# Score passes of two maps taken alternately, each in its own bank, and the dilated heads two at a time

## The chip, the cores and the metric

The kernel runs on one core of one Trainium2 chip. The metric is device time in microseconds (us) of one execution. Five engines work side by side and are told apart by their names in the profile: PE (TensorE, with PEld for its weight loads), DVE (VectorE), ACT (ScalarE), POOL (GpSimd) and SP (SyncE, which issues DMAs).

## The reference, cut to what matters

Two transformer blocks over 512 tokens of width 1024, in fp32. The first block holds, beside a feed-forward part, eight heads of ordinary causal attention ("mla" in the kernel) and eight "dilated" heads of width 64. The second block runs two layers; each has four heads of differential attention, where a head has two score maps of width 64 whose softmaxes are subtracted.

```python
def dilated_attention(q, k, v):              # 8 heads of 64, first block
    ...
    for window, dil in DIL_PATTERNS:         # the kernel folds the patterns into one additive mask
        ...
    w = jax.nn.softmax(jnp.stack(lses, axis=0), axis=0)
    out = jnp.sum(w[..., None] * jnp.stack(outs, axis=0).astype(jnp.float32), axis=0)
...
def diff_attention(q, k, v, lq1, lk1, lq2, lk2, subln_g, rel_bias, lam_init):   # 4 heads x 2 maps of 64, each layer
    ...
        logits = jnp.einsum('bqhmd,bkhmd->bhmqk', qb, k).astype(f32) + bias
        logits = jnp.where(dist >= 0, logits, NEG_INF_2)
        p = jax.nn.softmax(logits, axis=-1)
        attn = p[:, :, 0] - lam * p[:, :, 1]
        return jnp.einsum('bhqk,bkhe->bqhe', attn.astype(v.dtype), v)
```

## The kernel before

**Products in three passes.** An fp32 operand is split into a high part and the rest (`hi` and `lo`, `qh` and `ql`, `th` and `tl`), and a product is the sum of three matmuls: high by high, and high by low twice. L414 issues these three passes for one block of scores; L202 to L204 and L183 to L185 do the same for the linear layers.

**Scores.** The 512 queries are taken in four blocks of 128 (`i` = 0 to 3); block `i` needs the scores against the first 128(i+1) keys, so a pass has 128, 256, 384 or 512 columns. `softmax_block` takes a PSUM bank from a pool of two (`psc`), issues the three passes of one map into it, lets DVE add the mask and take the row maximum out of the bank (L417, `z<-psc`, which frees the bank), and then has ACT take the exponential. A dilated head has its q and k in 64 rows: `th` and `tl` hold two heads, the first in rows 0 to 63, the second in rows 64 to 127. A differential head holds its two maps in the same way. So these passes contract over 64 rows and use one half of the rows of the array (the profile prints 64*128 where a full matmul is 128*128). The mla heads contract over 96 rows.

**The order of work.** `attention` walks through the heads one after the other and through the four blocks of each; one step `b` issues the scores of block `b`, the transposes of the probabilities of block `b - 3` (`put_pt`, L430) and, one step later, the products with the values (`values`, L455) of a finished head. `weave` puts pieces of other work between the steps at given rates ("fill": projections, and sums for a modulation vector, `adacc`). In the first block the 16 heads are eight dilated ones and then eight mla ones; the 32 dilated steps lie at 134 to 245 us of the trace, the mla steps at 245 to 330 us. In the second block the four differential heads of a layer lie at 1133 to 1236 us and at 2051 to 2152 us, each step with both maps. The order of instructions on an engine is set by a scheduler when the program is built, from the order in the code and its own idea of when a bank or an input is ready; on the chip each engine's queue then has that order.

**Names.** `psc` score bank, `pmm` bank of the linear layers, `ptr` transposes, `po` values, `z` a block's scores in SBUF, `pt` transposed probabilities (two buffers for the dilated and mla heads), `lo<-raw,hi` the low parts of a weight piece (L161, on DVE or POOL), `relm` and `kc` the masks.

Of the kernel before, what the change touches and what calls it, by code (L numbers as in the profile page):

```python
# [18 lines left out]
P = 128  # L19
# [384 lines left out]
            self.x = [self.done[n] for n in (1, 5, 6, 2, 7, 3, 4)]  # L404


def softmax_block(net, mats, i, mask, scale):

    nc = net.nc
    n = (i + 1) * P  # L410
    q = slice(i * P, i * P + P)
    ps = net.ps_sc()
    for j, (l, r) in enumerate(mats):
        nc.tensor.matmul(ps[:, :n], l[:, q], r[:, :n], start=(j == 0), stop=(j == len(mats) - 1))  # L414
    z = net.zp.tile([P, T], F32, tag="z", name="z")
    nm, s = net.tiny(1, "nm"), net.tiny(1, "s")
    nc.vector.tensor_tensor_reduce(out=z[:, :n], in0=ps[:, :n], in1=mask[:, T - n:], scale=-scale, scalar=BIG,  # L417
                                   op0=ALU.add, op1=ALU.min, accum_out=nm)
    nc.scalar.activation(out=z[:, :n], in_=z[:, :n], func=AF.Exp, scale=-1.0, bias=nm, accum_out=s)
    r = net.tiny(1, "r")  # L420
    nc.vector.reciprocal(out=r, in_=s)
    return z, r
# [37 lines left out]
def mats3(qh, ql, kh, kl):  # L460
    return [(qh, kh), (qh, kl), (ql, kh)]


def attention(net, heads):


    n = NB * len(heads)
    zs, ends = {}, []
    for b in range(n + LAG + VLAG):
        if b == 0:  # L470
            heads[0].prepare()
        if b % NB == NB - 1 and b < n - 1:
            heads[b // NB + 1].prepare()
        if b < n:
            zs[b] = heads[b // NB].scores(b % NB)
        c = b - LAG
        if 0 <= c < n:
            h = heads[c // NB]
            if c % NB == 0:
                h.pt = h.new_pt()  # L480
            put_pt(net, zs.pop(c), c % NB, *h.pt)
        c -= VLAG
        if c >= 0 and c % NB == NB - 1:
            ends.append(heads[c // NB].output())
        for e in ends:
            next(e, None)
        yield
    for e in ends:
        for _ in e:
            pass  # L490
# [32 lines left out]
class Head64:  # L523
# [3 lines left out]
    def __init__(self, net, prep, mask, scale, v, out, then=None):  # L527
        self.net, self.prep, self.mask, self.scale, self.v, self.out = net, prep, mask, scale, v, out
        self.then = then

    def prepare(self):
        self.mats = self.prep()

    def scores(self, i):
        nc = self.net.nc
        z, r = softmax_block(self.net, self.mats, i, self.mask, self.scale)
        n = (i + 1) * P
        if i in ON_DVE:
            nc.vector.tensor_scalar(out=z[:, :n], in0=z[:, :n], scalar1=r, scalar2=None, op0=ALU.mult)
        elif i in SCALE_POOL:  # L540
            nc.gpsimd.tensor_tensor(out=z[:, :n], in0=z[:, :n], in1=r.to_broadcast([P, n]), op=ALU.mult)
        else:
            nc.scalar.activation(out=z[:, :n], in_=z[:, :n], func=AF.Identity, scale=r)
        return z
# [289 lines left out]
def first_body(net):  # L834
# [64 lines left out]
    with ExitStack() as c2:  # L899
# [295 lines left out]
        def shared_keys():  # L1195
# [4 lines left out]
            for kh, kl in ks:  # L1200
# [4 lines left out]

        net.share = SHARE[0]
        half1 = 4 * NB - 1
        weave(attention(net, dilated(0) + dilated(1) + mla(ks)),
              (half1, chain(dil_keys(1), dil_values(1)), RATES[0],
               mods, ADA_RATES[0]),  # L1210
              (half1 + 1, chain(mla_queries(), mla_keys(), shared_keys()), RATES[1], mods, ADA_RATES[1]),
# [225 lines left out]
class HeadDiff:  # L1437
# [6 lines left out]
    def new_pt(self):  # L1444
        return new_pt(self.net)

    def prepare(self):
        pass

    def scores(self, i):  # L1450
        net, nc = self.net, self.net.nc
        n = (i + 1) * P
        ms = []
        for m in range(2):
            r = slice(64 * m, 64 * m + 64)
            ms.append(softmax_block(net, mats3(*(t[r, :] for t in self.qk())), i, self.masks[:, m, :], 1.0))
        (z0, r0), (z1, r1) = ms
        nc.vector.tensor_scalar(out=r1, in0=r1, scalar1=self.nlam, scalar2=None, op0=ALU.mult)
        nc.scalar.activation(out=z1[:, :n], in_=z1[:, :n], func=AF.Identity, scale=r1)
# [24 lines left out]
def mixer(net, l, x, norm, M, nlam, gsub, sp8, nsp8, wl):  # L1484
# [37 lines left out]
    def da():  # L1522
        hs = []
        for hh in range(4):
# [8 lines left out]
                return vs[hp][0][kb // 2][:, c], vs[hp][1][kb // 2][:, c]  # L1533

            hs.append(HeadDiff(net, lambda hh=hh: qk["q", hh] + qk["k", hh], M[hh], nlam, v, out))
        return attention(net, hs)

    def scaled(c0, name, out):
        for j, ps in net.lin_fm(W[:, c0:c0 + 256], KD, 256, x):
# [199 lines left out]
```

## Time and profile before

| | |
|---|---|
| median of three executions | 2595.83 us (2595.31 to 2596.23) |
| profiled execution | 2595.03 us, of which the span of the trace is 2593.2 us |
| PE busy | 2512.7 us, 97% of the span |
| DVE busy | 1903.2 us, 73% |
| ACT busy | 1214.8 us, 47% |
| POOL busy | 269.2 us, 10% |
| mean granted TensorE clock | 0.986 of full speed |

The page's busy times are unions of instruction spans. A matmul's span reaches to the end of its results, while the next one starts earlier, so PE counts as busy also where it only drains; how close PE is to its limit has to be read from the distances between the starts of its matmuls.

### The profile page before, as it was taken

What the parts mean: (1) busy time and instruction counts of PE and PEld (TensorE: products, weight loads), DVE (VectorE), ACT (ScalarE), POOL (GpSimd) and SP (SyncE); (2) the same over time, 40 slices, a digit from 0 to 9 for tenths busy, and PEclk for the clock granted to TensorE, in tenths of its full rate; (3) what the DMA queues carried; (4) which work ended last, traced back from release to release, by engine and by line L of the source; (5) the groups of instructions that cost most, each with busy time, mean ns of one, the idle gap of its engine ahead of it and who ended that gap; (6) DMA issues with size and microseconds to landing.
All of it is one profiled execution on the core that took longest, in us unless ns stands there. A gap on an engine that the chain in (4) does not pass through costs nothing.

```text
span 2593.2 us, 38138 instructions
## 1 busy us (share of the span) xinstructions
PE 2512.7 (97%) x15288; PEld 2188.8 (84%) x15288; DVE 1903.2 (73%) x2860; ACT 1214.8 (47%) x1804; POOL 269.2 (10%) x246
## 2 busy tenths in 40 slices
PE   5999989999989999999999999999999999999998
PEld 4886768788879999887789999799998877899998
DVE  8788786555578877656688777788776566897775
ACT  4367644233355444445455444554444455544443
POOL 3256320000000000022200000000000222000000
PEclk9999989999999999999999999999999999999999
DMA  8432253333223333331223333233333421233332
GB/s 254 121 105 71 78 152 102 123 97 94 79 80 114 98 103 101 113 115 50 73 82 106 99 107 98 74 118 103 104 106 98 122 66 52 76 117 98 106 110 70
DMA packets 318774, 261.62 MB, mean 101 GB/s; under 512 B 10203, under 2 KB 310619, under 8 KB 318596
## 3 DMA queue, kind: packets, MB, share of 16 engines
q1 hardware_dynamic: 313184, 250.98, 31.4%
q10 hardware_dynamic: 5412, 8.20, 1.0%
q8 instruction: 120, 1.97, 0.3%
q14 instruction: 58, 0.48, 0.1%
HBM read 257.03 MB, written 4.74 MB: 101 GB/s over the span
## 4 chain that ended last, share of the span: by engine, by line
PE 49%; DVE 2%; ACT 1%; POOL 1%; issue 0%; DMA 0%; DVEq 0%; POOLq 0%; ACTq 0%; SPq 0%
PE ptr L183 4%; PE ptr L184 4%; PE ptr L185 4%; PE pmm L245 4%; PE pmm L247 4%; PE pmm L246 4%; PE pmm L183 3%; PE pmm L185 3%; PE pmm L184 3%; PE po L245 2%; PE po L246 2%; PE po L247 2%; PE psc L247 2%; PE psc L246 2%; PE psc L245 2%; PE pmm L203 1%
## 5 line engine op out<-in xcount | busy, mean ns | idle before, releaser
L157 ACT ACTIVATE hi<-raw 128x1024 fp32r<-128x1024 f32 (+3 forms) x434 | 448.0, 1033 | 545.5 <-PE pmm L184 171.1
L161 DVE TENSOR_TENSOR lo<-raw,hi 128x1024 fp32r<-128x1024 f32 (+2 forms) x402 | 482.4, 1201 | 219.4 <-ACT hi L157 213.6
L247 PE MATMUL pmm<-gh,lo 128*128 128x256 f32 x1344 | 378.8, 282 | 5.7 <-DVE lo L161 5.6
L245 PE MATMUL pmm<-gh,hi 128*128 128x256 f32 x1344 | 379.9, 283 | 3.1 <-ACT hi L157 2.5
L246 PE MATMUL pmm<-gl,hi 128*128 128x256 f32 x1344 | 378.3, 282 | 0.0
L183 PE MATMUL ptr<-uh,hi 128*128 128x512 f32 x832 | 330.2, 397 | 0.2 <-ACT hi L157 0.2
L184 PE MATMUL ptr<-ul,hi 128*128 128x512 f32 x832 | 329.3, 396 | 0.0
L185 PE MATMUL ptr<-uh,lo 128*128 128x512 f32 x832 | 329.0, 395 | 0.0
L253 POOL TENSOR_TENSOR rp<-var,neghalf 128x4 f32<-128x4 f32 (+2 forms) x46 | 56.8, 1236 | 1989.8 <-DVE var L258 1989.6
L245 PEld LDWEIGHTS pmm<-gh,hi 128*128 128x128 f32 x1344 | 258.4, 192 | 5.5 <-ACT hi L157 3.1
L247 PEld LDWEIGHTS pmm<-gh,lo 128*128 128x128 f32 x1344 | 254.0, 189 | 6.6 <-DVE lo L161 6.6
L246 PEld LDWEIGHTS pmm<-gl,hi 128*128 128x128 f32 x1344 | 254.3, 189 | 1.1
L183 PEld LDWEIGHTS ptr<-uh,hi 128*128 128x128 f32 x832 | 156.7, 188 | 37.4 <-ACT inv L308 0.8
L185 PEld LDWEIGHTS ptr<-uh,lo 128*128 128x128 f32 x832 | 156.3, 188 | 37.8
L184 PEld LDWEIGHTS ptr<-ul,hi 128*128 128x128 f32 x832 | 156.5, 188 | 35.9
L245 PE MATMUL po<-gh,hi 128*128 128x256 f32 x640 | 179.6, 281 | 1.7 <-ACT hi L157 1.7
L246 PE MATMUL po<-gl,hi 128*128 128x256 f32 x640 | 179.2, 280 | 0.0
L247 PE MATMUL po<-gh,lo 128*128 128x256 f32 x640 | 179.1, 280 | 0.0
L183 PE MATMUL pmm<-hh,hi 128*128 128x512 f32 x400 | 160.6, 403 | 6.2 <-ACT hh L761 3.3
L185 PE MATMUL pmm<-hh,lo 128*128 128x512 f32 x400 | 160.5, 402 | 3.8 <-DVE lo L161 3.8
L184 PE MATMUL pmm<-hl,hi 128*128 128x512 f32 x400 | 160.1, 401 | 0.0
L157 ACT ACTIVATE hi<-s 128x1024 fp32r<-128x1024 f32 x72 | 76.6, 1064 | 171.1 <-PE ptr L184 114.5
(411 smaller groups left out, 5841.4 us busy)
## 6 DMA issues: line engine op xcount, KB each, us to landing
raw<-in_ffn_gate SPq DMA_DIRECT2D x88, 512.0 KB, 3.6
raw<-in_ffn_up SPq DMA_DIRECT2D x88, 512.0 KB, 3.6
raw<-in_ffn_down SPq DMA_DIRECT2D x64, 512.0 KB, 3.4
raw<-in_w_in SPq DMA_DIRECT2D x60, 512.0 KB, 3.8
raw<-in_w_up SPq DMA_DIRECT2D x44, 512.0 KB, 3.8
wa<-in_w_ada SPq DMA_DIRECT2D x80, 256.0 KB, 3.0
raw<-in_ffn_down SPq DMA_DIRECT2D x32, 384.0 KB, 3.4
raw<-in_w_down SPq DMA_DIRECT2D x16, 512.0 KB, 3.4
```

What stands on the lines that cost most here:

```text
L157: nc.scalar.activation(out=hi, in_=v, func=AF.Copy)
L161: e.tensor_tensor(out=lo, in0=v, in1=hi.bitcast(F32), op=ALU.subtract)
L183: mm(ps, hi[:, k, c], xh, start=(k == 0), stop=False)
L184: mm(ps, hi[:, k, c], xl, start=False, stop=False)
L185: mm(ps, lo[:, k, c], xh, start=False, stop=(k == kt - 1))
L203: mm(ps[:, :n], xh[:, c], lo[:, k % kp, :], start=False, stop=False)
L245: mm(o, hi[:, k, c], xh[:, k, :], start=first, stop=False, skip_group_check=True)
L246: mm(o, hi[:, k, c], xl[:, k, :], start=False, stop=False, skip_group_check=True)
L247: mm(o, lo[:, k, c], xh[:, k, :], start=False, stop=(j == 1 and k == 3), skip_group_check=True)
L253: self.nc.gpsimd.tensor_tensor(out=r, in0=v, in1=self.neghalf[:, :n], op=ALU.pow)
```

## The change

`products` is new: it takes one bank for each map that it is given, and issues the first pass of every map, then the second pass of every map, then the third. `softmax_block` now gets a bank that is already filled. `attention` gets groups of heads in place of heads: a group's blocks are walked through together (block 0 of each head, then block 1 of each, ...), and all banks of the group's block are taken and filled at the step of its first head. A differential head is a group by itself with two maps; an mla head is a group by itself with one; the dilated heads form four groups of two. Number of passes, softmaxes, transposes and products with the values stay as they are, and so do the number of steps and the fill given to each.

```diff
-def softmax_block(net, mats, i, mask, scale):
+def products(net, i, *mats):
+
+
+    n = (i + 1) * P
+    q = slice(i * P, i * P + P)
+    banks = [net.ps_sc() for _ in mats]
+    for j, passes in enumerate(zip(*mats)):
+        for ps, (l, r) in zip(banks, passes):
+            net.nc.tensor.matmul(ps[:, :n], l[:, q], r[:, :n], start=(j == 0), stop=(j == len(mats[0]) - 1))
+    return banks
+
+
+def softmax_block(net, ps, i, mask, scale):
 
     nc = net.nc
     n = (i + 1) * P
-    q = slice(i * P, i * P + P)
-    ps = net.ps_sc()
-    for j, (l, r) in enumerate(mats):
-        nc.tensor.matmul(ps[:, :n], l[:, q], r[:, :n], start=(j == 0), stop=(j == len(mats) - 1))
     z = net.zp.tile([P, T], F32, tag="z", name="z")
...
-def attention(net, heads):
-
-
-    n = NB * len(heads)
+def attention(net, groups):
+
+
+
+    items = [(g, h, i) for g in groups for i in range(NB) for h in g]
+    later = dict(zip(groups, groups[1:]))
+    n = len(items)
     zs, ends = {}, []
+    for h in groups[0]:
+        h.prepare()
     for b in range(n + LAG + VLAG):
-        if b == 0:
-            heads[0].prepare()
-        if b % NB == NB - 1 and b < n - 1:
-            heads[b // NB + 1].prepare()
         if b < n:
-            zs[b] = heads[b // NB].scores(b % NB)
+            g, h, i = items[b]
+            if i == NB - 1 and h is g[-1]:
+                for other in later.get(g, ()):
+                    other.prepare()
+            if h is g[0]:
+                banks = products(net, i, *chain(*(o.maps() for o in g)))
+                for o in g:
+                    o.banks, banks = banks[:o.n_maps], banks[o.n_maps:]
+            zs[b] = h.scores(i)
         c = b - LAG
         if 0 <= c < n:
-            h = heads[c // NB]
-            if c % NB == 0:
+            _, h, i = items[c]
+            if i == 0:
                 h.pt = h.new_pt()
-            put_pt(net, zs.pop(c), c % NB, *h.pt)
+            put_pt(net, zs.pop(c), i, *h.pt)
         c -= VLAG
-        if c >= 0 and c % NB == NB - 1:
-            ends.append(heads[c // NB].output())
+        if c >= 0 and items[c][2] == NB - 1:
+            ends.append(items[c][1].output())
...
-        weave(attention(net, dilated(0) + dilated(1) + mla(ks)),
+        pairs = lambda hs: list(zip(hs[::2], hs[1::2]))
+        weave(attention(net, pairs(dilated(0)) + pairs(dilated(1)) + [(h,) for h in mla(ks)]),
...
+    def maps(self):
+        return [mats3(*(t[64 * m:64 * m + 64, :] for t in self.qk())) for m in range(2)]
...
-        ms = []
-        for m in range(2):
-            r = slice(64 * m, 64 * m + 64)
-            ms.append(softmax_block(net, mats3(*(t[r, :] for t in self.qk())), i, self.masks[:, m, :], 1.0))
+        ms = [softmax_block(net, self.banks[m], i, self.masks[:, m, :], 1.0) for m in range(2)]
...
-        return attention(net, hs)
+        return attention(net, [(h,) for h in hs])
```

What it does to the order of PE and DVE stands below at three places; the number behind a name tells buffers apart.

PE, second block, first layer, first differential head, 512 columns. Before, the three passes of map 0 into one bank and then those of map 1 into the other, in one piece:

```order
L414 MATMUL psc_10830<-kh_10479,qh_10436 128x512
L414 MATMUL psc_10830<-kl_10480,qh_10436 128x512
L414 MATMUL psc_10830<-kh_10479,ql_10437 128x512
L414 MATMUL psc_10841<-kh_10479,qh_10436 128x512
L414 MATMUL psc_10841<-kl_10480,qh_10436 128x512
L414 MATMUL psc_10841<-kh_10479,ql_10437 128x512
```

After:

```order
L415 MATMUL psc_10830<-kh_10479,qh_10436 128x512
L415 MATMUL psc_10831<-kh_10479,qh_10436 128x512
L415 MATMUL psc_10830<-kl_10480,qh_10436 128x512
L415 MATMUL psc_10831<-kl_10480,qh_10436 128x512
L415 MATMUL psc_10830<-kh_10479,ql_10437 128x512
L415 MATMUL psc_10831<-kh_10479,ql_10437 128x512
```

The six passes stood together before and stand together now; only the order among them has changed.

PE, first block, dilated stage, third head (the first of the second pair). Before, its block of 256 columns and, after three transposes, its block of 384; the fourth head's blocks stand about 80 rows further down:

```order
L414 MATMUL psc_1750<-th_1620,th_1611 128x256
L414 MATMUL psc_1750<-tl_1621,th_1611 128x256
L414 MATMUL psc_1750<-th_1620,tl_1612 128x256
L430 MATMUL ptr_1762<-ident_110,z_1592 128x128 x3
L414 MATMUL psc_1767<-th_1620,th_1611 128x384
L414 MATMUL psc_1767<-tl_1621,th_1611 128x384
L414 MATMUL psc_1767<-th_1620,tl_1612 128x384
```

After, the third and the fourth head's blocks of 256 columns in two banks, with the transposes and the values behind them:

```order
L415 MATMUL psc_1760<-th_1621,th_1612 128x256
L415 MATMUL psc_1761<-th_1621,th_1612 128x256
L415 MATMUL psc_1760<-tl_1622,th_1612 128x256
L415 MATMUL psc_1761<-tl_1622,th_1612 128x256
L415 MATMUL psc_1760<-th_1621,tl_1613 128x256
L415 MATMUL psc_1761<-th_1621,tl_1613 128x256
L438 MATMUL ptr_1776<-ident_110,z_1625 128x128 x4
L463 MATMUL po_1782<-pt_1422,vd_1072 64x512
```

Each head's three passes were a piece of their own; now the six passes of two heads are one piece, and the next block of the same head no longer stands right behind.

DVE, first block, dilated stage, fifth head, in the mla queries' fill. Before, the read of the head's second bank (`psc_2222`, 256 columns), with what stands ahead of it:

```order
L1093 TENSOR_SCALAR vr6_2161<-ss9_2159 128x3
L726 TENSOR_TENSOR sw_2170<-pmm_2144,g_mla_q_pe_s_588 128x3x16
L1091 TENSOR_SCALAR vr6_2161<-vr6_2161 128x3
L726 TENSOR_TENSOR sw_2170<-pmm_2144,g_mla_q_pe_s_588 128x3x16
L417 ISA z_2226,nm_2227<-psc_2222,kc_605 128x256
L417 ISA nm_2227 128x1
```

After, the read of the bank that the sixth head's first block has taken beside the fifth's (`psc_2120`), with what stands ahead of and behind it; the fifth head's bank (`psc_2119`) is read 13 rows earlier:

```order
L1115 TENSOR_SCALAR vr6_2157<-ss9_2155 128x3
L748 TENSOR_TENSOR sw_2166<-pmm_2140,g_mla_q_pe_s_588 128x3x16
L1113 TENSOR_SCALAR vr6_2157<-vr6_2157 128x3
L748 TENSOR_TENSOR sw_2166<-pmm_2140,g_mla_q_pe_s_588 128x3x16
L161 TENSOR_TENSOR lo_2181<-raw_2178,hi_2180 128x576
L1129 TENSOR_TENSOR t1_2164<-t1_2164,sw_2166 128x3x32
L425 ISA z_2218,nm_2219<-psc_2120,kc_605 128x128
L425 ISA nm_2219 128x1
L161 TENSOR_TENSOR lo_2384<-raw_2381,hi_2383 128x768
```

The read of the pair's second bank now stands behind a low-part subtraction (`lo`) and the fill's small steps, 13 rows behind the read of its first, and both banks are needed for the pair's next block.

## Rows read from the trace of the kernel before

**Rows 1.** Page, part 1: engine, busy us, share of the span, instructions.

```profile
PE 2512.7 (97%) x15288; PEld 2188.8 (84%) x15288; DVE 1903.2 (73%) x2860; ACT 1214.8 (47%) x1804; POOL 269.2 (10%) x246
```

**Rows 2.** Windows: stretch and length in us, busy us of each engine, PEclk, DMA share, GB/s.

```profile
134.00:245.00 111.00, 108.92 (x654) 84.12 (x653) 91.38 (x339) 75.37 (x188) 72.48 (x103) 1.00 0.29 93
160.00:220.00 60.00, 59.32 (x380) 47.97 (x380) 51.75 (x196) 39.45 (x95) 45.00 (x66) 1.00 0.41 134
189.00:220.00 31.00, 30.32 (x190) 24.30 (x189) 25.95 (x118) 20.03 (x47) 27.10 (x46) 1.00 0.32 107
1133.00:1208.00 75.00, 74.95 (x427) 60.60 (x427) 43.72 (x119) 41.97 (x89) 22.56 (x10) 1.00 0.27 78
1208.00:1236.00 28.00, 24.07 (x94) 16.45 (x93) 21.70 (x55) 19.25 (x40) 8.71 (x7) 0.82 0.07 20
```

**Rows 3.** Timeline of PE, second block, both maps: start, duration in us, line, out<-in, form, count.

```profile
1153.47 0.50 PE L414 MATMUL psc<-kh,qh 64*128 64x512 f32 x2
...
1154.04 0.40 PE L414 MATMUL psc<-kh,ql 64*128 64x512 f32 x2
1154.37 0.33 PE L430 MATMUL ptr<-ident,z 128*128 128x128 f32 x1
```

**Rows 4.** Timeline of PE, one dilated head's block of 512 columns and its neighbours.

```profile
141.85 0.29 PE L204 MATMUL pmm<-hi,hl 128*128 128x288 f32 x1
142.07 0.50 PE L414 MATMUL psc<-th 64*128 64x512 f32 x1
142.41 0.39 PE L414 MATMUL psc<-tl,th 64*128 64x512 f32 x1
142.64 0.39 PE L414 MATMUL psc<-th,tl 64*128 64x512 f32 x1
142.97 0.55 PE L430 MATMUL ptr<-ident,z 128*128 128x128 f32 x3
```

**Rows 5.** Timeline of PE, one dilated head's block of 384 columns and its neighbours.

```profile
138.26 0.34 PE L414 MATMUL psc<-tl,th 64*128 64x384 f32 x1
138.44 0.33 PE L414 MATMUL psc<-th,tl 64*128 64x384 f32 x1
138.70 0.40 PE L202 MATMUL pmm<-hi,hh 128*128 128x288 f32 x1
138.94 0.29 PE L203 MATMUL pmm<-lo,hh 128*128 128x288 f32 x1
139.07 0.29 PE L204 MATMUL pmm<-hi,hl 128*128 128x288 f32 x1
```

**Rows 6.** Timeline of PE, dilated head, second and third pass of 256 columns.

```profile
147.87 0.28 PE L414 MATMUL psc<-tl,th 64*128 64x256 f32 x1
147.98 0.27 PE L414 MATMUL psc<-th,tl 64*128 64x256 f32 x1
```

**Rows 7.** Timeline of PE, dilated head, second and third pass of 128 columns.

```profile
161.12 0.27 PE L414 MATMUL psc<-tl,th 64*128 64x128 f32 x1
161.23 0.27 PE L414 MATMUL psc<-th,tl 64*128 64x128 f32 x1
```

**Rows 8.** Timeline of PE, end of the dilated stage, two heads' blocks side by side.

```profile
234.49 0.49 PE L414 MATMUL psc<-th 64*128 64x512 f32 x2
234.66 0.27 PE L414 MATMUL psc<-tl,th 64*128 64x128 f32 x1
```

**Rows 9.** Timeline of PE, second block, second head of the first layer, first passes of both maps.

```profile
1163.92 0.38 PE L414 MATMUL psc<-kh,qh 64*128 64x256 f32 x1
...
1164.59 0.38 PE L414 MATMUL psc<-kh,qh 64*128 64x256 f32 x1
```

**Rows 10.** Waits of PE, whole trace: what it waited for, us in total, times, longest.

```profile
PE psc L414 <- DVE nm L417: 5.8, 4, 2.6
```

**Rows 11.** Groups of DVE by form, 134 to 245 us: count, busy us, mean ns, idle before.

```profile
L161 DVE TENSOR_TENSOR lo<-raw,hi 128x1024 fp32r<-128x1024 f32 x5 | 6.3, 1266 | 0.1
...
L161 DVE TENSOR_TENSOR lo<-raw,hi 128x576 fp32r<-128x576 f32 x4 | 3.6, 888 | 0.2 <-ACT hi L157 0.2
```

More of the change, by code (lines that the diff above doesn't have):

```diff
@@ L529, in __init__ @@
         self.then = then
+    n_maps = 1
     def prepare(self):
         self.mats = self.prep()
+    def maps(self):
+        return [self.mats]
     def scores(self, i):
         nc = self.net.nc
-        z, r = softmax_block(self.net, self.mats, i, self.mask, self.scale)
+        z, r = softmax_block(self.net, *self.banks, i, self.mask, self.scale)
         n = (i + 1) * P
@@ L1445, in new_pt, with maps @@
         return new_pt(self.net)
+    n_maps = 2
     def prepare(self):
         pass
+    def maps(self):
+        return [mats3(*(t[64 * m:64 * m + 64, :] for t in self.qk())) for m in range(2)]
     def scores(self, i):
```

## The prediction, made before the changed kernel ran

> **What bounds the kernel now.** I read the page's part 1 first: PE is busy 97% of the span, DVE 73% [rows 1]. Then the windows of the stretches that the change touches. In the dilated stage (134 to 245 us) PE is busy 108.9 of 111 us with DVE at 91.4 and POOL at 72.5; in its middle, 160 to 220 us, PE has 59.3 of 60 us and DVE 51.8 (86%), and from 189 us on POOL has 27.1 of 31 [rows 2]. In the differential heads of the first layer PE is busy all but 0.05 us of 75 us up to 1208 us, and 24.1 of 28 in the tail after that, at a granted clock of 0.82 [rows 2]. So PE sets the pace in the dilated stage and in most of the differential one, and what counts is how far apart its matmuls start. For that I read the timeline of PE, and there the important thing is the count at a row's end: two passes in one row are two maps.
>
> **The differential heads: already side by side.** In the code before, map 0's three passes stand ahead of map 1's. Yet the trace shows two first passes of 512 columns within 0.50 us, and two third passes within 0.40; from the first start to the transpose behind, six passes take 1154.37 - 1153.47 = 0.90 us [rows 3]. One dilated head's three passes of 512 take 142.97 - 142.07 = 0.90 us too [rows 4]. Passes in the two halves of the rows run at the same time, and the first pass of map 1 did not wait for the second and third of map 0, though it was issued behind them. I counted the 32 blocks of the two layers: 23 run in pairs like this one, and the nine others are eight in the two tails, where PE is not the bound, and one in the middle. Alternating the issue therefore gains nothing in 23 blocks. The one in the middle, second head, 256 columns, has its maps 1164.59 - 1163.92 = 0.67 us apart [rows 9]; if they overlap after the change, that is 0.6 us. Between nothing and 0.67 I take 0.6, since 23 blocks of the same form do overlap. In the tails the order of DVE changes somewhat; the nearest row is PE's wait for the read of a score bank, 5.8 us in four waits, the longest 2.6 [rows 10]. So each tail may move by up to 2.6 us in either direction; I take zero, since no order there favours one sign.
>
> Here the Trainium skill says the opposite of the row. TensorE: Matmul & The Clock Gate (Part 3, The mechanism) states that matmuls keep program order in start and end, a strict FIFO in which only weight loads are pulled ahead. By that rule the six passes would have taken turns before, and the change would pay in all 32 blocks; the third rival gives the time. The rows of the pairs contradict it.
>
> **The dilated heads: what pairing removes.** A dilated head now runs alone in its half of the rows. The price of a pass is the distance between the second and third start: 0.11 us for 128 columns [rows 7], 0.11 to 0.12 for 256 [rows 6], 0.18 for 384 [rows 5], 0.23 for 512 [rows 4]. On top, every visit of PE to 64-row passes costs about 0.41 us: 0.22 from the wide matmul ahead to the first pass [rows 4], where wide ones of this width are 0.13 apart [rows 5], so 0.09; the first pass 0.34 instead of 0.23, so 0.11; the way out 0.33 instead of 0.23, so 0.10 [rows 4]; the next wide matmul 0.24 instead of 0.13, so 0.11 [rows 5].
>
> Before: 8 heads x 3 passes of each width, 24 x (0.11 + 0.12 + 0.18 + 0.23) = 15.4 us, less 0.33 for one block of 128 that already runs beside a block of 512 at the end of the stage [rows 8], so 15.0; and 30 visits (I counted them in the timeline; two are shared by two blocks).
>
> After, by the order of PE: of the 16 pairs, six stand whole in one visit (256, 384 and 512 of the second pair of heads, 384 and 512 of the third, 256 of the fourth); three blocks of 128 alternate but are split over two visits; the 384 of the fourth pair is split with one pass alone; six are still two separate pieces, because the scheduler saw the second bank come free late (five in two visits, the 128 of the second pair in three). Taking a side-by-side couple as one pass, that is 15 passes of 128, 18 of 256, 16 of 384 and 18 of 512: 1.65 + 2.16 + 2.88 + 4.14 = 10.8 us, in 6 + 6 + 2 + 13 = 27 visits.
>
> Saved on PE: 15.0 - 10.8 = 4.2 us of passes and 3 x 0.41 = 1.2 us of visits, 5.4 us. Nearly all lies in the second and third pair (about 2.4 us each), that is in 160 to 220 us.
>
> **What takes some of it back.** In that stretch DVE has 8.2 us free of 60 and POOL 3.9 of 31 [rows 2]. Their work does not shrink, and a pair's block needs both banks: the read of the second one now stands one step ahead of the next pair's passes instead of two, behind low-part subtractions of 0.89 to 1.27 us [rows 11]. When it is late, everything queued behind the pair's passes on PE waits too (the fill's projections, hence DVE's, ACT's and POOL's steps on them). No row shows this wait. Bounds: nothing lost, since the free time of DVE exceeds the saving; or all 5.4 us. I take 1.9, about a third, nearer to nothing because PE is the fuller engine there. The probabilities' buffers (two, now both in one pair's hands) cost nothing in the order: a pair's first transposes stand behind the values of the head that frees the buffer, with PE's other work around them. Softmaxes, transposes, values and DMAs are the same in number; the loads on SP only trade places with each other. After 245 us the work shifts earlier as a whole.
>
> Sum: -5.4 + 1.9 - 0.6 = -4.1 us. Against the profiled execution, span 2593.2 and 1.8 around it, 2595.0 - 4.1 = 2590.9; that execution lies 0.8 under the median, so 2591.7.
>
> **The rivals.** (1) Nothing is given back, and PE's idle time in the dilated stage (2.1 us of 111) goes too: -5.4 - 0.6 and up to -2.1, -6 to -8 us, 2588 to 2590. For it speaks that PE was the fuller engine; against it DVE's 86%. (2) Slower: the second bank's read. Twelve pairs follow another pair of the same heads; if each waited for one low-part subtraction of 1.27 us, that is +15.2, and against the 6.0 saved the kernel loses 9.2: 2605. It breaks even at 6.0 / 12 = 0.5 us a pair. Against it: the scheduler has spread six pairs apart just to avoid this, and PE's whole trace shows only four waits of that kind [rows 10]. (3) The differential maps did not really run together, and alternating is what makes them: three passes of each width saved in four blocks, 0.64 x 3 = 1.9 us a head, eight heads, 15.4 us on top: 2576. The 0.90 us for six passes speak against it [rows 3, 4]. (4) The change does what it says, but DVE and POOL set the pace in 160 to 220 us, and all but the edges is lost: 2595 to 2596.
>
> **How the numbers follow.** Forecast 0.50, rival 1 0.27, rival 2 0.08, rival 3 0.02, rival 4 0.13. 0.2% is 5.2 us, about what a measurement of this kernel can tell from no change: below 2590.6 and above 2601.0. Faster: rivals 1 and 3 and a small part of the forecast, 0.33. Slower: most of rival 2, 0.07. Same: 0.60. The range of 8 in 10 runs from 2587 (rival 1, with one tail gaining) to 2598 (rival 4, with one tail losing 2.6).
>
> **What would show it.** Right: in 1133 to 1208 us the six passes still take 0.90 us at 512 columns and the stretch keeps its length within 1 us; in the dilated stage rows of 512 columns with count 2, and the mla steps starting about 3.5 us earlier. Wrong: PE waits for the read of a score bank (L425) inside the dilated stage that sum to over 3 us; or a differential stage shorter by several us, which would mean that the overlap before was not what I read. The forecast also fails if the tails move by more than 2.6 us each.

## The result, and the profile after

The changed kernel is slower: 2609.36 us median of four runs (2604.85 to 2613.1) against 2595.84 (2595.31 to 2596.23), ratio 1.0057 with a 95% interval of 1.0044 to 1.0069. The medians are 13.5 us apart, and the new one lies outside the range of 2587 to 2598. A second series gave 1.0050 (1.0032 to 1.0068).

Part 1 of the page after (before: [rows 1]):

```profile
PE 2520.6 (97%) x15288; PEld 2191.7 (84%) x15288; DVE 1906.0 (73%) x2860; ACT 1214.4 (47%) x1804; POOL 264.9 (10%) x246
```

This execution was the slowest of the four; a second trace of the same kernel has a span of 2605.6 us, and loses at the same places. The shares on the page say nothing of what happened: PE is at 97% as before. So I cut the span where the change acts, by marks that exist in both kernels. The dilated stage goes from the first 64-row pass to the first projection matmul that needs all eight dilated heads (L183); a differential stage has a body, up to the first pass of its last head, and a tail from there to its last 64-row pass. Windows of the kernel before (columns as in [rows 2]: stretch, length, busy time of each engine, granted clock of PE, DMA share, GB/s):

```profile
134.13:252.43 118.30, 116.22 (x696) 89.22 (x695) 97.00 (x360) 82.01 (x206) 73.29 (x104) 1.00 0.28 90
1134.32:1208.89 74.57, 74.52 (x423) 60.24 (x422) 44.60 (x122) 41.80 (x91) 22.44 (x10) 1.00 0.27 78
1208.89:1235.45 26.56, 22.63 (x85) 15.39 (x85) 20.26 (x50) 17.81 (x37) 8.51 (x6) 0.81 0.07 21
2051.81:2125.79 73.98, 73.98 (x423) 59.90 (x422) 44.51 (x123) 41.80 (x91) 22.10 (x10) 1.00 0.27 79
2125.79:2151.60 25.81, 21.69 (x86) 14.20 (x85) 19.00 (x49) 17.92 (x37) 8.44 (x7) 0.87 0.07 21
```

The same five of the changed kernel, and two shorter ones inside the first:

```profile
133.66:259.70 126.04, 119.26 (x697) 90.40 (x696) 101.94 (x363) 80.78 (x205) 76.43 (x107) 0.95 0.29 90
1141.47:1218.81 77.34, 75.24 (x424) 60.23 (x423) 45.75 (x122) 41.70 (x90) 22.41 (x10) 1.00 0.27 78
1218.81:1246.92 28.11, 24.32 (x82) 16.20 (x83) 19.45 (x50) 18.06 (x38) 7.46 (x6) 0.76 0.04 13
2065.55:2141.30 75.75, 74.51 (x423) 59.95 (x422) 44.93 (x122) 42.21 (x90) 22.08 (x10) 1.00 0.26 77
2141.30:2169.62 28.32, 23.64 (x86) 15.10 (x85) 19.47 (x50) 18.12 (x37) 8.47 (x7) 0.82 0.07 19
...
217.00:222.00 5.00, 5.00 (x21) 4.02 (x20) 4.12 (x18) 2.71 (x9) 4.69 (x9) 0.66 0.32 105
244.00:256.00 12.00, 11.66 (x42) 8.06 (x43) 8.43 (x27) 6.34 (x18) 2.09 (x2) 0.57 0.21 66
```

The dilated stage is 126.0 instead of 118.3 us long, +7.7. Three parts make this up. PE's idle time (length less busy) went from 2.1 to 6.8 us, +4.7 (8.4 in the second trace). The granted clock, 1.00 throughout before, is 0.66 and 0.57 of full speed in the two short stretches: part of each ran at 1.2 in place of 2.4 GHz, which costs at most 5.00 x 0.34 + 12.00 x 0.43 = 6.9 us. And the matmuls themselves: 119.26 - 6.9 = 112.4 us at full clock against 116.2, a saving of about 3.8. So the change did what it says, and gave back three times as much.

The differential stages lose 2.77 and 1.77 us in their bodies and 1.55 and 2.51 in their tails, 8.6 in all. Together 16.3 of the 18.1 us between the two spans; the remaining 1.8 lie in stretches whose instructions are the same.

The waits of PE between 134 and 256 us in the changed kernel (waiting line, what it waited for, us in total, times, longest):

```profile
PE pmm L202 <- DVE sw L748: 2.3, 2, 1.7
PE ptr L438 <- DVE tl L589: 1.6, 3, 0.8
PE psc L415 <- DVE nm L425: 1.4, 1, 1.4
```

Only one of these waits, 1.4 us, is for a score bank. The longest is for something else: the fill's projections wait until DVE (L748) has read their bank. PE around it and at the end of the last pair, in the changed kernel (start, duration, line, operands, count, idle time ahead and what ended it):

```profile
213.15 0.64 PE L415 MATMUL psc<-th 64*128 64x512 f32 x2
...
214.19 0.44 PE L438 MATMUL ptr<-ident,z 128*128 128x128 f32 x2
216.38 0.48 PE L202 MATMUL pmm<-hi,lkh 128*128 128x512 f32 x1 [1.75 <-DVE sw L748]
...
217.65 0.63 PE L204 MATMUL pmm<-hi,lkl 128*128 128x512 f32 x1
...
244.11 0.55 PE L438 MATMUL ptr<-ident,z 128*128 128x128 f32 x3 [0.79 <-DVE tl L589]
244.89 0.95 PE L415 MATMUL psc<-kh,th 96*128 96x128 f32 x2 [0.23 <-ACT kh L588]
```

The pair of 512-column blocks runs side by side, six passes in 1.04 us (213.15 to 214.19), as meant. Then PE stands still for 1.75 us, and soon after, from 217.65 on, its passes take 0.63 us: the clock has fallen. The same happens at 244 us, where the last pair's two heads end together and PE has only transposes and the short first blocks of the next head to run.

In the second trace the clock falls at the pair's end too (246.0 to 252.8 us), but not at 217 us. There PE is through sooner, and then waits for DVE:

```profile
223.62 0.47 PE L202 MATMUL pmm<-hi,lkh 128*128 128x512 f32 x1 [1.26 <-DVE r L429]
```

The first trace has no such wait there, and the stage is as long in one as in the other (126.04 and 126.07 us). So of the up to 1.7 us (5.00 x 0.34) that the half clock at 217 us costs, 1.26 would have gone to this wait.

What DVE's L748 stands behind at 213 to 216 us is seen on ACT, in the second trace of the changed kernel:

```profile
214.98 0.61 ACT L565 ACTIVATE z<-z,r 128x384 f32<-128x384 f32 x1 [0.23 <-DVE r L429]
215.50 0.40 ACT L1106 ACTIVATE sq<-pmm,rp 128x192 f32<-128x192 f32 x1
```

Both heads' exponentials (L427, at 212.60 and 214.06 us) and scalings (L565, at 213.54 and 214.98 us) of 384 columns come first, one behind the other, and only then the fill's square (L1106), for which DVE waits 0.99 us before it can go on to L748.

### The profile page after: what moved, and what is told of

Same layout as the page of the kernel before. It is cut to its first block, busy times and chain, and to the rows that moved or that the text cites. A ratio compares the mean times of both kernels' runs of the same rounds, so it can differ in the third digit from the quotient of the medians.

```text
span 2611.3 us, 38134 instructions
## 1 busy us (share of the span) xinstructions
PE 2520.6 (97%) x15288; PEld 2191.7 (84%) x15288; DVE 1906.0 (73%) x2860; ACT 1214.4 (47%) x1804; POOL 264.9 (10%) x246
## 4 chain that ended last, share of the span: by engine, by line
PE 71%; DVE 6%; ACT 2%; issue 1%; DMA 1%; POOL 1%; DVEq 0%; POOLq 0%; ACTq 0%; SPq 0%
PE ptr L183 7%; PE ptr L184 7%; PE ptr L185 7%; PE pmm L183 5%; PE pmm L185 5%; PE pmm L184 5%; PE pmm L245 5%; PE pmm L247 5%; PE pmm L246 5%; PE po L245 3%; PE po L246 3%; PE po L247 3%; PE psc L247 2%; PE psc L246 2%; PE psc L245 2%; DVE lo L161 1%
## 5 line engine op out<-in xcount | busy, mean ns | idle before, releaser
L183 PE MATMUL ptr<-uh,hi 128*128 128x512 f32 x832 | 330.2, 397 | 0.2 <-ACT hi L157 0.2
L245 PEld LDWEIGHTS pmm<-gh,hi 128*128 128x128 f32 x1344 | 258.9, 193 | 7.8 <-ACT hi L157 3.6
L247 PEld LDWEIGHTS pmm<-gh,lo 128*128 128x128 f32 x1344 | 255.0, 190 | 5.9 <-DVE lo L161 5.7
L183 PEld LDWEIGHTS ptr<-uh,hi 128*128 128x128 f32 x832 | 156.6, 188 | 37.6 <-ACT inv L308 0.8
L183 PE MATMUL pmm<-hh,hi 128*128 128x512 f32 x400 | 160.6, 402 | 6.2 <-ACT hh L783 3.3
```

The source lines that it names most:

```text
L183: mm(ps, hi[:, k, c], xh, start=(k == 0), stop=False)
L245: mm(o, hi[:, k, c], xh[:, k, :], start=first, stop=False, skip_group_check=True)
L247: mm(o, lo[:, k, c], xh[:, k, :], start=False, stop=(j == 1 and k == 3), skip_group_check=True)
```

## The experiments

All kernels were measured beside runs of the kernel before, with a ratio and its 95% interval as on record; the ratio can differ a little from the quotient of the medians. Beside these kernels the kernel before took, at the median, 2595.86 us (changed again, differential maps only, pairs only, pairs in turn), 2595.45 us (one pass later, first two and first three pairs, pairs filled) and 2597.73 us (the last two rows). The last three columns are from one trace of each: the time at which the first projection of the finished dilated heads starts, and the lengths of body and tail of the two differential stages.

| kernel | median us | ratio | projection at | layer 0 | layer 1 |
|---|---|---|---|---|---|
| before | 2595.84 | | 252.4 | 74.57 + 26.56 | 73.98 + 25.81 |
| changed | 2609.36 | 1.0057 (1.0044 to 1.0069) | 259.7 | 77.34 + 28.11 | 75.75 + 28.32 |
| changed, again | 2608.98 | 1.0050 (1.0032 to 1.0068) | 258.9 | 77.33 + 28.21 | 75.73 + 26.41 |
| differential maps only | 2603.29 | 1.0032 (1.0019 to 1.0046) | 252.4 | 77.33 + 28.19 | 75.74 + 28.14 |
| differential maps, one pass later | 2603.93 | 1.0035 (1.0024 to 1.0047) | 255.0 | 77.35 + 28.22 | 75.75 + 27.70 |
| pairs only | 2604.18 | 1.0030 (1.0016 to 1.0043) | 258.9 | 74.57 + 26.15 | 73.96 + 25.83 |
| pairs in turn | 2602.09 | 1.0023 (1.0010 to 1.0036) | 263.1 | 74.56 + 25.95 | 73.97 + 24.64 |
| first two pairs only | 2600.07 | 1.0020 (1.0009 to 1.0031) | 256.6 | 74.56 + 26.03 | 73.97 + 27.50 |
| first three pairs only | 2599.82 | 1.0020 (1.0011 to 1.0029) | 254.6 | 74.58 + 26.91 | 73.98 + 27.71 |
| pairs, filled | 2602.20 | 1.0023 (1.0013 to 1.0033) | 256.8 | 74.57 + 26.29 | 73.96 + 25.45 |
| before, tails filled | 2593.23 | 0.9988 (0.9979 to 0.9996) | 252.0 | 74.56 + 27.54 | 73.97 + 23.83 |
| changed, filled | 2605.09 | 1.0031 (1.0018 to 1.0044) | 255.1 | 78.90 + 26.16 | 75.73 + 25.69 |

Where the dilated code is that of before, the projection starts between 252.0 and 255.0 us. The spread comes from what lies ahead of the dilated stage, whose instructions all these kernels share: in some executions the dilated stage begins at 131 us at half clock, in others at about 133, mostly at full. A difference of 3 us in that column says little, one of 6 does. The bodies repeat to 0.02 us, but for the last row's 78.90, where 3.4 us ran at half clock.

**The changed kernel again.** 

> The changed kernel once more, for a second trace. Theory one (the losses hang on the order of work): the same four places lose again, each within 1 us of the first trace: 236 to 250 us of before +7 (half clock at 245 to 255 us), 1150 to 1230 +4.3, 2070 to 2150 +4.3, about 2605 to 2613 in all. Rival (the half clock at 245 us is an accident of one execution): no half clock there in this trace, and the time nearer 2603.

The losses came at the same places: half clock at 246.0 to 252.8 us, the projection 6.5 us later than before, the first body to 0.01 us. Two things differ: the clock does not fall at 217 us, where PE waits instead, and the last tail takes 26.41 us after 28.32, with 3.4 us less of it at half clock. The rival falls.

**Each half alone.** The maps of the differential heads only, and the pairs only:

```diff
-        weave(attention(net, pairs(dilated(0)) + pairs(dilated(1)) + [(h,) for h in mla(ks)]),
+        weave(attention(net, [(h,) for h in dilated(0) + dilated(1) + mla(ks)]),
```

```diff
-    n_maps = 2
+    n_maps = 0
...
-        return [mats3(*(t[64 * m:64 * m + 64, :] for t in self.qk())) for m in range(2)]
+        return []
...
-        ms = [softmax_block(net, self.banks[m], i, self.masks[:, m, :], 1.0) for m in range(2)]
+        ms = []
+        for m in range(2):
+            mats = mats3(*(t[64 * m:64 * m + 64, :] for t in self.qk()))
+            ms.append(softmax_block(net, *products(net, i, mats), i, self.masks[:, m, :], 1.0))
```

> Only the two maps of a differential head alternate; dilated heads are taken one at a time as before. Theory one (a pass of the second map that waits for its bank holds back the first map's second and third pass, which stand behind it): +4.3 us in each of the two differential stages, nothing before 1133 us, about 2604.5. Rival (the differential stages lose only because the pairs shifted what runs beside them): within 2 us of the kernel before, 2594 to 2598.

> Only the dilated heads are taken two at a time with alternating passes; the two maps of a differential head are issued one after the other as before. Theory one (the pair's order makes TensorE wait at 213 to 216 us and 243 to 245 us, and the clock falls to half behind these waits): -1 us of passes, +7 us at 213 to 255 us, about 2602. Rival (the pairs lose nothing, all of it is the alternated maps): 2591 to 2596.

Measured +7.4 and +8.3 us. Each half loses by itself, and each only in its own stage: the maps leave the projection at 252.4 us, the pairs leave the bodies at 74.57 and 73.96. Both rivals fall, and the two losses add up, within the intervals, to that of the whole.

**What the alternated maps cost.** The second head's block of 256 columns, maps issued in turn (the kernel with pairs only):

```profile
1170.37 0.38 PE L415 MATMUL psc<-kh,qh 64*128 64x256 f32 x1
...
1170.71 0.28 PE L415 MATMUL psc<-kh,ql 64*128 64x256 f32 x1
1171.03 0.38 PE L415 MATMUL psc<-kh,qh 64*128 64x256 f32 x1
...
1171.58 0.55 PE L438 MATMUL ptr<-ident,z 128*128 128x128 f32 x3
```

and alternating (the kernel with the differential maps only):

```profile
1163.96 0.38 PE L415 MATMUL psc<-kh,qh 64*128 64x256 f32 x1
1164.84 0.38 PE L415 MATMUL psc<-kh,qh 64*128 64x256 f32 x1 [0.50 <-DVE nm L425]
...
1165.06 0.39 PE L415 MATMUL psc<-kh,ql 64*128 64x256 f32 x2
1165.38 0.55 PE L438 MATMUL ptr<-ident,z 128*128 128x128 f32 x3
```

In turn, the second map's bank comes free 0.66 us into the block and map 0 is through by then. Alternating, the second map's first pass waits for the bank with map 0's second and third pass behind it. The overlap that I had hoped for here came, but from the first pass to the transposes it now takes 1.42 us and not 1.21. My theory was that this hold-up is the loss. The rows do not bear it out: from the first pass into the freed bank to the transposes it is 0.54 us alternating (1164.84 to 1165.38) and 0.55 us in turn (1171.03 to 1171.58). The 0.21 us are the bank's, which DVE frees 0.88 us into the block and not 0.66. The next kernel issues the passes as first, first, second, first, second, second, so that only one pass stands behind the wait:

```diff
-    for j, passes in enumerate(zip(*mats)):
-        for ps, (l, r) in zip(banks, passes):
-            net.nc.tensor.matmul(ps[:, :n], l[:, q], r[:, :n], start=(j == 0), stop=(j == len(mats[0]) - 1))
+    last = len(mats[0]) - 1
+    for j, m in sorted(((j, m) for m in range(len(mats)) for j in range(last + 1)), key=lambda p: p[0] + 1.5 * p[1]):
+        l, r = mats[m][j]
+        net.nc.tensor.matmul(banks[m][:, :n], l[:, q], r[:, :n], start=(j == 0), stop=(j == last))
```

> The two maps of a differential head alternate, but one pass later: first, first, second, first, second, second; dilated heads one at a time as before. Only the first map's third pass stands behind the second map's wait for its bank. VectorE's row of instructions in the differential stages is nearly that of the alternating kernel (32 rows differ), not that of before (135 differ). Theory one (passes of the first map are held back behind the wait): half of the alternated maps' loss or less, 2596 to 2600, the stretch from 1133 to 1206 us at most +0.8. Rival (what loses is that the planner, seeing the first map end later, puts VectorE's read of it behind other work): the same loss as alternating, +1.7 by 1206 us, about 2603.

The rival holds: 2603.93 us and bodies of 77.35 and 75.75, the same to 0.02, and the block above takes 1.41 us in it. What the two kernels have nearly in common is the order of DVE. DVE with the maps in turn (pairs only):

```profile
1172.55 0.35 DVE L1488 SCALAR_TENSOR_TENSOR z<-z,r 128x128 f32<-128x128 f32 x1 [0.53 <-ACT z L1487]
1172.81 0.42 DVE L425 CUSTOM_DVE_ANT_0 z<-psc,relm 128x256 f32<-128x256 f32 x1
...
1173.15 0.48 DVE L1546 SCALAR_TENSOR_TENSOR vl<-pmm,rp,vh 128x256 fp32r<-128x256 f32 x1
...
1174.03 0.42 DVE L425 CUSTOM_DVE_ANT_0 z<-psc,relm 128x256 f32<-128x256 f32 x1
```

and alternating (differential maps only):

```profile
1166.35 0.35 DVE L1485 SCALAR_TENSOR_TENSOR z<-z,r 128x128 f32<-128x128 f32 x1 [0.53 <-ACT z L1484]
1166.71 0.48 DVE L1543 SCALAR_TENSOR_TENSOR vl<-pmm,rp,vh 128x256 fp32r<-128x256 f32 x1
1167.11 0.42 DVE L425 CUSTOM_DVE_ANT_0 z<-psc,relm 128x256 f32<-128x256 f32 x1
...
1167.45 0.55 DVE L448 TENSOR_TENSOR ptl<-ptr,pth 128x384 fp32r<-128x384 f32 x1
...
1168.29 0.40 DVE L425 CUSTOM_DVE_ANT_0 z<-psc,relm 128x256 f32<-128x256 f32 x1
```

The read of map 0 (L425) now stands behind the value's low part, and the read of map 1 behind the probabilities' low part. Counted from L1488 and L1485, the second read starts 1.94 us later instead of 1.48. Map 0's scores had been ready for 1.66 us by then (the third passes started at 1165.06 and took 0.39, the read came at 1167.11): the queue's order delays the read, not PE. The likely reason, which no run tests, is that the scheduler sees map 0 end later when its passes alternate, and gives DVE's earlier place to other work. Each delayed read holds a bank for the next blocks. The 512 block, 0.91 us long in turn, takes 1.28 alternating, and the last head's first pass waits 0.79 us for a bank, which it does not in the kernel with pairs only. The read that it waits for now stands behind a low part and two steps of other work (L1566); DVE, then PE (differential maps only):

```profile
1208.63 1.23 DVE L161 TENSOR_TENSOR lo<-raw,hi 128x1024 fp32r<-128x1024 f32 x1 [2.18 <-PE psc L415]
...
1210.97 0.68 DVE L425 CUSTOM_DVE_ANT_0 z<-psc,relm 128x512 f32<-128x512 f32 x1
```

```profile
1211.71 0.32 PE L415 MATMUL psc<-kh,qh 64*128 64x128 f32 x1 [0.79 <-DVE nm L425]
```

Not all of the loss is a bank's. Compared pass by pass with the kernel with pairs only, the body of layer 0 falls behind in four steps: by 0.2 us at the block of 256 columns, 0.6 after the block of 512, 1.7 after the sums of a finished head's squares (L267), and 2.8 at the last head's first pass. Layer 1 has two steps, 0.75 us at the block of 256 and 1.8 after the sums. So in each body about 1 us is lost at the sums, where PE waits for the square on ACT. ACT with the maps in turn (pairs only):

```profile
1184.35 0.63 ACT L1504 ACTIVATE sq<-o 128x512 f32<-128x512 f32 x1
1184.89 0.71 ACT L1487 ACTIVATE z<-z,r 128x512 f32<-128x512 f32 x1
```

and alternating (differential maps only), with PE behind it:

```profile
1179.60 0.72 ACT L1484 ACTIVATE z<-z,r 128x512 f32<-128x512 f32 x1
1180.23 0.61 ACT L1501 ACTIVATE sq<-o 128x512 f32<-128x512 f32 x1
```

```profile
1180.90 1.05 PE L267 MATMUL ptr<-ones,sq 128*128 128x1 f32 x8 [0.82 <-ACT sq L1501]
```

The square stood ahead of the scaling of 512 columns and now stands behind it. That the new order on DVE and ACT is the cause rests on these readings and on the equal loss of the two kernels; a kernel with the maps alternating and the old order of both was not tried. Nor was a third score bank.

The tails issue their passes map by map in both kernels, and lose too. In layer 0 they last 25.95 to 26.91 us in the unfilled traces with the maps in turn and 28.11 to 28.22 alternating; in layer 1 the two kinds overlap. The alternating ones run 13.7 us of the first tail at half clock, those in turn 6.8 to 10.2; what in the tail's changed order starts it stays open.

**What the pairs cost.** First without alternation, each head's three passes issued at its own step:

```diff
-    n_maps = 1
+    n_maps = 0
...
     def maps(self):
-        return [self.mats]
+        return []
...
-        z, r = softmax_block(self.net, *self.banks, i, self.mask, self.scale)
+        z, r = softmax_block(self.net, *products(self.net, i, self.mats), i, self.mask, self.scale)
```

> The dilated heads are taken two at a time, but each head's three passes are issued together, not alternating with the other's; the differential heads as before. Theory one (what loses is the order of the blocks of two heads and where the next heads are prepared): within 2 us of the kernel with alternating pairs, about 2602. Rival (what loses is the alternation, a pass that waits for its bank in front of the other head's passes): better than the alternating pairs by 3 us or more, 2592 to 2598.

2602.09 us, not apart from the alternating pairs' 2604.18 by more than the intervals allow: theory one. Its dilated stage:

```profile
130.80:263.09 132.29, 126.22 (x697) 95.33 (x696) 104.36 (x363) 81.37 (x205) 77.28 (x107) 0.94 0.28 86
```

Idle 6.1 us, like the 6.8 with alternation and unlike the 2.1 of before. So the idle time comes with the order of two heads together, not with the alternating passes. At full clock the busy time would be 126.22 - 132.29 x 0.06 = 118.3 us, against 119.14 - 125.98 x 0.05 = 112.8 with alternating pairs, so alternating does spare PE work in this order, about 5.5 us. Then fewer pairs, two and three:

```diff
-        weave(attention(net, pairs(dilated(0)) + pairs(dilated(1)) + [(h,) for h in mla(ks)]),
+        weave(attention(net, pairs(dilated(0)) + [(h,) for h in dilated(1) + mla(ks)]),
```

```diff
-        weave(attention(net, pairs(dilated(0)) + pairs(dilated(1)) + [(h,) for h in mla(ks)]),
+        weave(attention(net, pairs(dilated(0) + dilated(1)[:2]) + [(h,) for h in dilated(1)[2:] + mla(ks)]),
```

> Only the first four dilated heads are taken in pairs, the last four one at a time; differential heads as before. Theory one (most of the loss hangs on the end of the last pair, where two heads end together with no other work left and the clock falls): no half clock at 244 us and no wait at 236 to 246 us, -2 to +2 against before, 2594 to 2598. Rival (pairs lose wherever they stand, by waits for VectorE): +3 to +4 by 250 us, about 2600.

> The first six dilated heads in pairs, the last two one at a time; differential heads as before. Theory one: the last two heads end as before, no half clock at 244 us; the wait at 213 us stays, 2595 to 2599. Rival (the loss moves with the waits for VectorE and comes at another place): about 2602, as with four pairs.

Both lost 4.4 to 4.6 us. For two pairs that is the rival's number, for three it lies between the theories. In neither is there a half clock at 244 us, as theory one has it. With three pairs the end of the stage looks like this, where the changed kernel has 0.57:

```profile
243.00:255.00 12.00, 12.00 (x62) 7.25 (x61) 9.26 (x31) 10.42 (x28) 1.34 (x1) 1.00 0.07 23
```

So part of the pairs' loss hangs on the last pair's end: in traces that enter the stage at the same time (133.05 and 132.93 us), the projection starts 4.3 us sooner with three pairs than with four (the medians, 4.4 us apart, have intervals that overlap). The other part is there with fewer pairs too: PE idles 5.3 us of the stage with two pairs and 121.55 - 115.52 = 6.0 us with three (133.05 to 254.60 us), and with three the clock still falls at 217 us. To see whether the clock has a price of its own I put twelve unread matmuls where the last pair ends:

```diff
+            if len(groups) > 4 and h is groups[4][0] and i < 2:
+                l, r = groups[3][0].mats[0]
+                ps = net.ps_mm()
+                for j in range(6):
+                    net.nc.tensor.matmul(ps, l[:, :P], r, start=(j == 0), stop=(j == 5))
```

> As the kernel with four alternating pairs, with twelve matmuls of 512 columns more that nobody reads, put between the last pair's last blocks and the first blocks of the next heads (240 to 248 us); 12 x 0.23 = 2.8 us of extra work. Theory one (the clock falls there because TensorE has little to stream; that costs 5.1 us of the pairs' loss): no half clock at 244 to 255 us, the k-th instruction at 260 us is 2 to 3 us earlier than with the pairs alone, about 2601. Rival (the clock falls whatever TensorE does there): 2.8 us later, about 2607.

The end of the stage, pairs only:

```profile
236.00:258.91 22.91, 21.61 (x86) 13.09 (x84) 14.87 (x44) 14.40 (x37) 6.35 (x8) 0.78 0.18 57
```

and filled:

```profile
236.00:256.82 20.82, 20.82 (x100) 12.28 (x100) 14.73 (x42) 15.38 (x39) 5.05 (x8) 1.00 0.24 69
```

With 2.8 us more to do, PE is through 2.1 us sooner, at full clock. The fall of the clock at this place is a cost of its own and follows what PE has to do: all four traces with four pairs and nothing filled in have it, the two with the filling do not. Over the whole stage these two traces are equally long (125.94 and 125.98 us), since the filled one ran at half clock from 151.3 to 158.1 us, where the other did not; why, stays open. (The whole kernel, 2602.20, is not apart from the 2604.18 unfilled by more than the intervals.)

**The tails filled.** The tails ran partly at half clock before the change already, [rows 2]. Ten unread matmuls behind the last head's first block, where PE waits, in the kernel before, and both fillings in the changed one:

```diff
+        if i == 0 and self.fill:
+            t = self.qk()
+            ps = net.ps_mm()
+            for j in range(self.fill):
+                nc.tensor.matmul(ps, t[2][:, :P], t[0], start=(j == 0), stop=(j == self.fill - 1))
...
+        hs[-1].fill = 10
```

> The kernel before, with ten matmuls of 512 columns more that nobody reads in each of the two differential stages, behind the first block of the last head, where TensorE waits 2.55 us for VectorE (10 x 0.23 = 2.3 us). Theory one (the clock falls to half behind that wait, and this, 5.1 us at 1211 us and 3.4 us at 2129 us, is a cost of its own): no half clock in the two tails, 4 to 8 us less, 2588 to 2592. Rival (the clock follows something else, or the waits that set the pace there only grow as TensorE gets faster): 2594 to 2600.

> The changed kernel with both fillings: twelve unread matmuls of 512 columns at the end of the last pair and ten behind the first block of the last differential head in each layer. Theory one (of the change's loss about 5 us at the pair's end and 1.7 us more in each tail than before are half clock, and filling takes back that and what the tails lost before too): no half clock at 244 to 255 us and none or little in the tails, about 2598 to 2602. Rival: as the changed kernel, 2606 to 2612.

The kernel before gains 0.12% by the ratio: 2593.23 us against 2597.73 in its series, interval 0.9979 to 0.9996, only just clear of no change. It is the one version here that beats both kernels. Its two tails:

```profile
1208.04:1235.58 27.54, 24.25 (x95) 16.16 (x95) 20.21 (x50) 17.94 (x37) 8.54 (x6) 0.88 0.07 20
2126.41:2150.24 23.83, 21.27 (x95) 14.55 (x95) 18.98 (x49) 17.83 (x37) 8.04 (x7) 1.00 0.08 23
```

In the second the half clock is gone and 2.0 us with it; in the first it came later, 6.8 instead of 10.2 us long, and the tail is 1.0 us longer, so theory one holds for one tail. The changed kernel filled, 2605.09 us and 1.0031, lies between theory one's 2598 to 2602 and the rival's 2606 to 2612, and its interval reaches into both: no half clock at 244 us, 6.8 and 3.4 us of it left in the tails, and still a loss.

## Why the prediction was wrong

**The differential heads.** That the six passes already ran side by side was right; after, at 512 columns:

```profile
1160.62 0.50 PE L415 MATMUL psc<-kh,qh 64*128 64x512 f32 x2
...
1161.51 0.33 PE L438 MATMUL ptr<-ident,z 128*128 128x128 f32 x1
```

0.89 us, as 0.90 in [rows 3]. The step that failed is the next one, "Alternating the issue therefore gains nothing in 23 blocks", read as costs nothing. I named the one block whose maps stood apart [rows 9], and counted it as 0.6 us to gain. That gap was a wait for a bank, and the bank was late because of DVE. After the change the maps overlap there, but DVE frees the bank later still and the block takes 0.21 us more; and the scheduler's new order of DVE and ACT delayed the reads of banks and a square behind it. I looked at the order of DVE for the tails and took zero; in the bodies I did not look. The term "-0.6, tails 0" measured +2.77 and +1.77 in the bodies and +1.55 and +2.51 in the tails (+1.65 and +0.60 in the second trace; each tail within the 2.6 that I had allowed, but with the sign that I had declined to choose).

**The saving on PE.** 5.4 us forecast, 3.8 measured (3.6 in the second trace: 117.67 us busy, less 126.07 x 0.04 for a clock of 0.96). The kind was right: in the rows at 213 us six passes of 512 columns take 1.04 us.

**The give-back.** 1.9 us forecast within 0 to 5.4; PE's idle time rose by 4.7, inside the bounds and near the upper one, and by 6.3 in the second trace, above it. I priced one mechanism, the second bank's read, and its wait came to only 1.4 us. Most of the rest is the fill's and the transposes' waits for DVE. Two blocks of the same size in a row put two reads, two exponentials and two scalings next to each other on DVE and ACT, and the fill's steps stand behind both, as in the rows of ACT. My bound "all 5.4 us" treated the saving as the most that can be lost; but a longer wait is not limited by what the passes saved.

**The clock.** This is the missing term, up to 6.9 us in the dilated stage of the first trace, of which up to 5.2 (12.00 x 0.43) at the last pair's end. I had its rows: the tails at 0.82 in [rows 2] against 1.00 in the dilated stage. I read them as a property of the tails and not as what follows when PE waits or has only short work. No rival held it. Rival 2 gave 2605 and "slower", to which I had given 0.07, but by a wait for score banks at twelve pairs, which is not what the trace shows.

So, of the pointers under "What would show it": the rows with count 2 came; the mla steps start 0.4 us earlier (244.89 for 245.29) and not 3.5, and run into the half clock; the sum of waits for L425 in the dilated stage stayed under 3 us, and still the forecast failed, since it did not watch the other waits; the stretch up to the last differential head is 2.8 us longer, not within 1.

## What to carry to other kernels

When PE sets the pace at full clock, a change of order is not free because it costs no instruction. Check, on DVE's and ACT's queues too, which operation now stands ahead of each read that frees a bank and of each result that PE waits for. Before giving several heads a common end, ask what PE runs while both chains drain: a gap there is paid once as idle time and again as half clock on the work behind it. And where such a gap can't be closed, matmuls that nobody reads can be worth more than they cost, as in the second tail of the kernel before.

## What the runs showed of the hardware

In both traces of the changed kernel an operation of two elements in each partition took as long as a large one beside it. POOL, then DVE, in the changed kernel:

```profile
207.37 2.37 POOL L161 TENSOR_TENSOR lo<-raw,hi 128x1024 fp32r<-128x1024 f32 x1
```

```profile
207.41 2.35 DVE L1115 TENSOR_SCALAR vr<-ss 128x2 f32<-128x2 f32 x1
```

The median of that DVE line is 0.16 us; this one started 0.04 us after POOL's subtraction and ended 0.02 us after it. The trace of before has such places too, though not this one: at 358.42 us a DVE operation of four elements in each partition (L1368, median 0.16 us) took 2.27 us beside a subtraction of the same size on POOL. The Trainium skill (SBUF — State Buffer, SBUF: two separate sides) says that VectorE and GpSimd share one pair of ports as an exclusive lock: between a GpSimd operation and a VectorE one in a two-port mode (or with two inputs in SBUF, where the GpSimd one reads SBUF), the first to start holds the ports for its whole length and the other is blocked. The trace agrees, 2.35 us beside 2.37; in which mode the DVE operation ran no row shows. Here it stopped DVE for 2.2 us just ahead of the two 384 blocks' reads, and PE's first wait for L748, 0.58 us at 210.25 us, comes behind it. The long wait does not hang on it: the kernel with pairs in turn has no such stop and waits 0.55 and 1.79 us for L748 (at 218.12 and 221.54 us), and the kernel with the first two pairs has one (2.35 us at 210.9 us) and no wait for L748 over 0.35 us.
